# Neighbourhood-attention heads: four single score banks, forms built in quarters, and a fixed TensorE order

## The chip, the cores and the metric

The kernel runs on one core of a Trainium2 chip. The metric is the device time of one execution in microseconds (us); lower is better. The engines that matter here are TensorE (PE), VectorE (DVE), ScalarE (ACT), GpSimd (POOL) and SyncE's DMA queue (SP).

## The reference

A two-layer encoder on x of 1 x 1024 x 1024 in f32. Each layer projects the normalised x once, feeds three groups of token mixers (6 heads of multi-head latent attention, called MLA; 6 heads of 2-D neighbourhood attention; 4 differential heads), gates their outputs, joins them and projects back. The change lies in the neighbourhood heads:

```python
def neighborhood_attention(q, k, v, rpb, scale):        # 64 x 16 grid, window 8 x 16 keys
    ...
    def one(r):
        r0 = jnp.clip(r - kr // 2, 0, rows - kr)
        q_r = lax.dynamic_index_in_dim(qg, r, axis=1, keepdims=False)
        k_r = lax.dynamic_slice_in_dim(kg, r0, kr, axis=1)[:, :, col_idx]
        v_r = lax.dynamic_slice_in_dim(vg, r0, kr, axis=1)[:, :, col_idx]
        ...
        s = jnp.einsum('bchd,brcjhd->bhcrj', q_r, k_r, preferred_element_type=jnp.float32) * scale
        s = s + bias.transpose(0, 2, 1, 3)[None].astype(jnp.float32)
        p = jax.nn.softmax(s.reshape(B, H, GRID_W, kr * kc), axis=-1).reshape(B, H, GRID_W, kr, kc)
        return jnp.einsum('bhcrj,brcjhd->bchd', p.astype(v.dtype), v_r)
```

## The kernel before, in words

Each layer runs latent and differential projections, the differential heads and gates, the neighbourhood projections, the **neighbourhood stage** (6 heads), the MLA stage (6 heads) and the output projection. In the neighbourhood stage a head has 8 tiles of 128 queries; a tile looks at 2 or 3 chunks of 128 keys (`NA_CHUNKS`), so that its score is 128 x 256 or 128 x 384.

The steps of a tile, with their lines before the change:
- **Score** (L1047, L1048): two matmuls into PSUM, because the keys are kept as a high and a low part.
- **Softmax**: DVE adds the bias and takes the minimum of the negated score in one pass (L1052), ACT takes the exponential and its sum (L1053), DVE the reciprocal (L1055), POOL multiplies (L1056).
- **Turn**: PE transposes the probabilities chunk by chunk (L677, in `transpose_plain`) into a T tile in PSUM, and ACT copies it to SBUF (L140, in `copy_act`).
- **Value products** (L1075): after every odd tile, for the pair of tiles that ends there, into an O tile. After tile 7, `finish` (L1084) multiplies them into the gate on DVE.

Ahead of a head stand its **forms**, the transposed queries and keys: four groups of 4 transposes into an F tile (L1018 for the two query halves, L1032 for the two key halves). A query half is finished by ACT (L1019) and then DVE (L1020), a key half by ACT (L140) and then DVE (L1034). A DVE copy (L1027) prepares the keys. `na_table` (L992) loads a head's bias table and prepares it on POOL.

The PSUM tiles: S (`psS`) is two tiles of 1024 columns, each two banks of 512; T is two tiles of one bank, F one and O one, eight banks in all. A score takes a whole S tile, so two scores are in rotation.

What sets the order: the program lists its steps by position, one position per tile (`at`, `run_events`): a score stands `ahead` = 3 positions before its tile, a head's forms `lead` = 4 before the head's first tile and its table `tlead` = 6. From that source order the tile framework's scheduler, with its own estimate of times, decides the order in which each engine gets its instructions; engines run them in that order. `chain(fn)` (L653) makes a step wait in the schedule behind the step chained last, which fixes TensorE's order to the source's; before the change the differential heads use it and the neighbourhood heads don't. `mla_setup` (L1107), with two loads of w_uq (L1114) and their high and low parts on DVE (L1120, L1121), belongs to the MLA stage, and the scheduler puts it among the neighbourhood heads' first tiles. Its two loads share one raw buffer, so the second starts when the first one's DVE work is done.

Of the kernel before, what the change touches and what calls it, by code (L numbers as in the profile page):

```python
# [27 lines left out]
    T=2,  # L28
    hl=(1, 3, 5, 7, 9, 11, 13, 15),
    start="x0 x1 x2 x3 a7 w0 x4 x5 x6 x7 a0 a1 w3 a2 w1 a3 a4 w2 a5 a6", ada="vvvvvvvg", xs=(), hi="A", ks=(0, 1, 7, 2, 3, 4, 5, 6),  # L30
    na=dict(lead=4, tlead=6, ahead=3, delay=0.0, step=0.0),
    late=((0, 8, 0, 12, 4), (0, 0, 0, 8, 0)),
    next=dict(banks="FOFOFOFO", lo=(0, 1, 2, 3)),
    norms=(((0, 2), "V"), ((2, 2), "G")), ropes=((0, 2), (2, 2)), nas=(4, 5), vafter=2,
# [9 lines left out]
def hybrid_encoder_kernel(  # L44
# [81 lines left out]
    def psF():  # L126
        return T(ps_1, "F", [128, 512], F32, bufs=1) if OPT["T"] < 3 else psT()
# [4 lines left out]
    def f(ap):  # L132
        return ap.bitcast(F32)
# [5 lines left out]
    def copy_act(o, i, scale=1.0):  # L139
        A.activation(o, i, AF.Copy, scale=scale)  # L140
# [321 lines left out]
    for l in range(depth):  # L462
# [208 lines left out]
                fn()  # L671
            events.clear()

        def transpose_plain(src_cols, dst, n, act):
            pt = psT()
            for i in range(n):
                ins = PE.transpose(pt[:, i * 128:(i + 1) * 128], src_cols(i), ident)  # L677
            pv = pt[:, 0:n * 128].rearrange("p (k n) -> p k n", n=128)
            if act:
                copy_act(dst, pv)  # L680
            else:
                V.tensor_copy(dst, pv)
            return ins

        def transpose_split(src_cols, hi4, lo4, n):

# [317 lines left out]
            G.tensor_tensor(ti, te, cmask.rearrange("p (d x) -> p d x", x=8).unsqueeze(2).to_broadcast([128, 3, 16, 8]), ALU.add)  # L1004
            return t[:, 384:768], t[:, 0:384]

        def na_forms(h, part=(0, 1)):
            e = h % 2
            hs = slice(h * 64, (h + 1) * 64)
            m, o = (64, 0) if e else (0, 64)  # L1010
            gq = vT[l][m:m + 64, 40:41]
            q, khi, klo = (forms[:, 3 * e + i] for i in range(3))
            ps_ = slice((h // 2) * 128, (h // 2 + 1) * 128)
            for th in range(2 if 0 in part else 0):
                ns = slice(th * 512, (th + 1) * 512)
                ps = psF()
                for t in range(4):
                    PE.transpose(ps[:, t * 128:(t + 1) * 128], nq[:, th * 4 + t, ps_], ident)  # L1018
                A.activation(q[m:m + 64, ns], ps[m:m + 64], AF.Copy, scale=gq)  # L1019
                V.scalar_tensor_tensor(q[o:o + 64, ns], ps[m:m + 64], gq, f(q[m:m + 64, ns]), ALU.mult, ALU.subtract)  # L1020
            if 1 not in part:
                return
            if h == 0:
                kn = rawtile([128, 1024]).rearrange("p (t h d) -> p t h d", h=2, d=64)
            else:
                kn = PTf[e][:, 6:8].rearrange("p a (t h d) -> p (a t) h d", h=2, d=64)
            V.tensor_copy(kn, nk[:, :, hs].unsqueeze(2).to_broadcast([128, 8, 2, 64]))  # L1027
            for th in range(2):
                ns = slice(th * 512, (th + 1) * 512)
                ps = psF()  # L1030
                for t in range(4):
                    PE.transpose(ps[:, t * 128:(t + 1) * 128], kn[:, th * 4 + t].rearrange("p h d -> p (h d)"), ident)  # L1032
                copy_act(khi[:, ns], ps)
                V.tensor_tensor(klo[:, ns], ps, f(khi[:, ns]), ALU.subtract)  # L1034

        def na_item(h, p):
            e, qb, tq = h % 2, p // 4, p % 4
            c0, n = NA_CHUNKS[p]
            w = n * 128
            q, khi, klo = (forms[:, 3 * e + i] for i in range(3))  # L1040
            box = {}

            def first():
                te, ti = na_tabs[h]
                ps = psS()[:, 0:w]
                ks = slice(c0 * 128, c0 * 128 + w)
# [12 lines left out]
                box["p"] = pb  # L1059

            def second():
                pb = box["p"]
                qs = slice(tq * 128, (tq + 1) * 128)
                transpose_plain(lambda i: pb[:, i * 128:(i + 1) * 128], PTf[qb][:, 0:n, qs], n, True)

            def third():

                if p == 1:
                    obox["na", h] = psO()
                O = obox["na", h][:, p // 2 * 128:(p // 2 + 1) * 128]  # L1070
                for i in range(3):
                    for t in (p - 1, p):
                        c, m = NA_CHUNKS[t]
                        if i < m:
                            PE.matmul(O[t % 2 * 64:t % 2 * 64 + 64], nv[:, c + i, h * 64:(h + 1) * 64],  # L1075
                                      PTf[qb][:, i, t % 4 * 128:(t % 4 + 1) * 128], start=(i == 0), stop=(i == m - 1),
                                      skip_group_check=True)

            def finish():
                m = 64 * e  # L1080
                g = sg[m:m + 64, 3 + h // 2].rearrange("p (t two n) -> p two t n", two=2, n=128)
                for half in range(2):
                    O = obox["na", h][half * 64:half * 64 + 64].rearrange("p (t n) -> p t n", n=128)
                    V.tensor_tensor(g[:, half], g[:, half], O, ALU.mult)  # L1084

            return first, second, ([third] if p % 2 else []) + ([finish] if p == 7 else [])

        def nv_side(tt):
            nonlocal forms
            if tt == OPT["nas"][0]:  # L1090
                forms = T(bp, "R0", [128, 8, 1024], F32R)
                na_forms(0, (0,))
            if tt == OPT["nas"][1]:
                na_forms(0, (1,))
# [317 lines left out]
```

## Time and profile before

| | us |
|---|---|
| runs | 1796.34, 1795.14, 1791.98 |
| median of the runs | 1795.14 |
| profiled execution, its own time | 1793.4 |
| its span in the trace | 1789.4 |
| PE busy | 1627.4 (91%) |
| DVE busy | 1305.3 (73%) |
| ACT busy | 902.0 (50%) |
| POOL busy | 782.5 (44%) |

The profiled execution's time is 4.0 us above its span and 1.7 us below the median. The busy shares are averages over all stages. The neighbourhood stage begins with the first score at 526.23 us in layer 0 and at 1393.31 us in layer 1; the first turns of heads 0, 1 and 5 lie at 533.33, 546.40 and 604.00 us in layer 0. A row of the timeline gives start, duration, engine, line and tiles, and in brackets the idle time of the engine before it and the instruction that ended that idle time.

### The profile page before, as it was taken

What the parts mean: (1) busy time and instruction counts of PE and PEld (TensorE: products, weight loads), DVE (VectorE), ACT (ScalarE), POOL (GpSimd) and SP (SyncE); (2) the same over time, 40 slices, a digit from 0 to 9 for tenths busy, and PEclk for the clock granted to TensorE, in tenths of its full rate; (3) what the DMA queues carried; (4) which work ended last, traced back from release to release, by engine and by line L of the source; (5) the groups of instructions that cost most, each with busy time, mean ns of one, the idle gap of its engine ahead of it and who ended that gap; (6) DMA issues with size and microseconds to landing.
All of it is one profiled execution on the core that took longest, in us unless ns stands there. A gap on an engine that the chain in (4) does not pass through costs nothing. (4 is left out here: it accounts for less than half of the span.)

```text
span 1789.4 us, 27407 instructions
## 1 busy us (share of the span) xinstructions
PE 1627.4 (91%) x10028; PEld 1376.8 (77%) x10028; DVE 1305.3 (73%) x2634; ACT 902.0 (50%) x1906; POOL 782.5 (44%) x759
## 2 busy tenths in 40 slices
PE   3999899989989899989998979899899889999998
PEld 2978677768876689878878877777689667897876
DVE  6889877875887589995576477778665666899732
ACT  5622577772127577653342226778511575776500
POOL 4532345544236544473225034455324364456532
PEclk8999899999989999999999999999999999999999
DMA  9335000103333000131232320001032130022032
GB/s 294 99 108 177 14 25 13 48 1 98 116 73 50 36 12 13 36 93 34 83 111 71 90 89 24 13 25 36 25 108 48 21 76 1 13 48 71 13 107 81
DMA packets 135497, 111.68 MB, mean 62 GB/s; under 512 B 32894, under 2 KB 118980, under 8 KB 134852
## 3 DMA queue, kind: packets, MB, share of 16 engines
q1 hardware_dynamic: 119596, 100.33, 19.7%
q0 software_dynamic: 12480, 6.29, 2.2%
q10 hardware_dynamic: 3288, 3.33, 0.9%
q8 instruction: 79, 1.29, 0.3%
q14 instruction: 54, 0.44, 0.1%
HBM read 92.10 MB, written 21.02 MB: 63 GB/s over the span
## 5 line engine op out<-in xcount | busy, mean ns | idle before, releaser
L659 PE MATMUL F<-R,Pb 128*128 128x512 f32 x766 | 232.2, 418 | 15.3 <-ACT sg L140 15.3
L140 ACT ACTIVATE R<-T 128x512 fp32r<-128x512 f32 (+2 forms) x288 | 153.5, 551 | 93.1 <-PE T L689 67.8
L659 PEld LDWEIGHTS F<-R,Pb 128*128 128x128 f32 x766 | 139.9, 195 | 51.4 <-ACT sg L140 22.7
L770 DVE TENSOR_REDUCE sm<-S 128x1 f32<-128x1024 f32 x128 | 153.5, 1217 | 18.4 <-PE S L765 17.2
L1220 POOL TENSOR_SCALAR Pb<-Pb,sm 128x1024 f32<-128x1024 f32 x96 | 109.2, 1138 | 131.8 <-DVE sm L1216 82.1
L692 DVE TENSOR_TENSOR R<-T,R 128x512 fp32r<-128x512 f32 x192 | 128.8, 682 | 24.8 <-ACT R L140 23.4
L1218 ACT ACTIVATE Pb<-S,sm,rs_q 128x1024 f32<-128x1024 f32 x96 | 115.5, 1203 | 40.2 <-DVE sm L1216 34.9
L1238 PE MATMUL O<-R,nd 128*128 128x256 f32 x768 | 120.5, 293 | 8.7 <-DVE R L692 8.1
L1215 DVE TENSOR_REDUCE sm<-S 128x1 f32<-128x1024 f32 x96 | 116.5, 1214 | 8.1 <-PE S L1212 7.7
L689 PE MATMUL T<-ident,Pb 128*128 128x128 f32 x768 | 111.7, 276 | 5.5 <-DVE R L692 5.2
L1238 PEld LDWEIGHTS O<-R,nd 128*128 128x128 f32 x768 | 102.5, 191 | 15.7 <-DVE R L692 11.7
L1344 POOL TENSOR_TENSOR raw<-sg,raw 128x512 fp32r<-128x512 f32 x32 | 50.0, 1562 | 121.0 <-DVE raw L1343 121.0
L689 PEld LDWEIGHTS T<-ident,Pb 128*128 128x128 f32 x768 | 90.4, 143 | 12.1 <-issue 4.1
L772 ACT ACTIVATE nd<-S,sm 128x1024 f32<-128x1024 f32 x64 | 71.4, 1116 | 44.8 <-DVE sm L770 41.3
L776 POOL TENSOR_SCALAR nd<-nd,sm 128x1024 f32<-128x1024 f32 x48 | 58.9, 1228 | 79.3 <-DVE sm L774 76.3
L494 ACT ACTIVATE t<-T 128x512 f32<-128x512 f32 x32 | 19.2, 599 | 143.3 <-DVE n1k L974 68.3
L840 POOL TENSOR_TENSOR Pb<-raw,Pb 128x512 fp32r<-128x512 f32 x32 | 42.1, 1318 | 112.7 <-DVE Pb L839 47.9
L772 ACT ACTIVATE sg<-S,sm 128x1024 f32<-128x1024 f32 x64 | 71.3, 1114 | 29.1 <-DVE sm L770 17.9
L1210 PE MATMUL S<-R 128*128 128x512 f32 x192 | 85.2, 446 | 0.4
L1056 POOL TENSOR_SCALAR Pb<-Pb,sm 128x384 f32<-128x384 f32 (+1 forms) x96 | 53.6, 568 | 59.7 <-DVE sm L1055 48.7
L1211 PE MATMUL S<-R 128*128 128x512 f32 x192 | 78.0, 406 | 0.0
L1212 PE MATMUL S<-R 128*128 128x512 f32 x192 | 77.4, 405 | 0.0
(434 smaller groups left out, 4994.8 us busy)
## 6 DMA issues: line engine op xcount, KB each, us to landing
raw<-in_w_in_dram SPq DMA_DIRECT2D x32, 512.0 KB
t<-in_ada_w_dram SPq DMA_DIRECT2D x40, 256.0 KB
n1k<-in_w_out_dram SPq DMA_DIRECT2D x16, 512.0 KB
v_d<-n1k SPq DMA_DIRECT2D x16, 384.0 KB
nl<-in_ada_w_dram SPq DMA_DIRECT2D x24, 256.0 KB
nd<-v_d POOLq DMA_DIRECT2D x12, 512.0 KB, 5.1
R<-in_ada_w_dram SPq DMA_DIRECT2D x8, 512.0 KB
Pb<-in_x_dram SPq DMA_DIRECT2D x8, 512.0 KB
```

The costliest lines, as they stand in the source:

```text
L140: A.activation(o, i, AF.Copy, scale=scale)
L659: ins = fn()
L689: PE.transpose(pt[:, i * 128:(i + 1) * 128], src_cols(i), ident)
L692: V.tensor_tensor(lo4, pv, f(hi4), ALU.subtract)
L770: V.tensor_reduce(stt[:, m:m + 1], ps, AX.X, ALU.max, negate=True)
L772: A.activation(p, ps.rearrange("p (k n) -> p k n", k=8), AF.Exp, bias=stt[:, m:m + 1], accum_out=stt[:, 2 + m:3 + m])
L1210: PE.matmul(o, qhi[:, ts_], khi[:, ks], start=True, stop=False)
L1211: PE.matmul(o, qhi[:, ts_], klo[:, ks], start=False, stop=False)
L1215: V.tensor_reduce(stt[:, 0:1], ps, AX.X, ALU.max, negate=True)
L1218: A.activation(p, ps, AF.Exp, bias=stt[:, 3:4], scale=rs, accum_out=stt[:, 1:2])
L1220: mla["g"] = G.tensor_scalar(p, p, stt[:, 2:3], 0.0, ALU.mult, ALU.add)
L1238: PE.matmul(box["o"], mla[f"v{e}"][:, k], mla["PT"][b][:, hl, k], start=(k == 0 and hl == 0), stop=(k == 7 and hl == 1))
```

## The change

- **Score banks**: two S tiles are taken once for the stage and cut into four single banks of 512 columns; scores rotate through these (`na_s`). `ahead` goes from 3 to 4.
- **Forms in quarters**: `na_forms` builds one quarter per call (query half 0, query half 1, key half 0, key half 1). The quarters of heads 1 to 5 are listed 1.25 positions apart, the first 9 positions before the head's first tile (`lead` from 4 to 9); `tlead` goes from 6 to 10. Head 0's quarters stand where its forms stood.
- **Order**: the transposes of a turn, the scores, the value products and the quarters of heads 1 to 5 go through `chain`, so TensorE gets the whole stage in source order.
- `transpose_plain` loses a choice of engine that was always ACT here.

```diff
-    na=dict(lead=4, tlead=6, ahead=3, delay=0.0, step=0.0),
+    na=dict(lead=9, tlead=10, ahead=4, delay=0.0, step=0.0),
...
-        def transpose_plain(src_cols, dst, n, act):
+        def transpose_plain(src_cols, dst, n):
             pt = psT()
-            for i in range(n):
-                ins = PE.transpose(pt[:, i * 128:(i + 1) * 128], src_cols(i), ident)
...
+            def pe():
+                for i in range(n):
+                    ins = PE.transpose(pt[:, i * 128:(i + 1) * 128], src_cols(i), ident)
+                return ins
+
+            chain(pe)
+            copy_act(dst, pt[:, 0:n * 128].rearrange("p (k n) -> p k n", n=128))
...
-        def na_forms(h, part=(0, 1)):
+        def na_forms(h, side, th, order):
...
+            ns, ps = slice(th * 512, (th + 1) * 512), psF()
...
+            order(pe)
+            if side:
+                copy_act(khi[:, ns], ps)
+                V.tensor_tensor(klo[:, ns], ps, f(khi[:, ns]), ALU.subtract)
+            else:
                 A.activation(q[m:m + 64, ns], ps[m:m + 64], AF.Copy, scale=gq)
                 V.scalar_tensor_tensor(q[o:o + 64, ns], ps[m:m + 64], gq, f(q[m:m + 64, ns]), ALU.mult, ALU.subtract)
...
-                ps = psS()[:, 0:w]
+                ps = na_s()[:, 0:w]
...
-                PE.matmul(ps, q[:, p * 128:(p + 1) * 128], khi[:, ks], start=True, stop=False)
-                PE.matmul(ps, q[:, p * 128:(p + 1) * 128], klo[:, ks], start=False, stop=True)
+                def pe():
+                    PE.matmul(ps, q[:, p * 128:(p + 1) * 128], khi[:, ks], start=True, stop=False)
+                    return PE.matmul(ps, q[:, p * 128:(p + 1) * 128], klo[:, ks], start=False, stop=True)
+
+                chain(pe)
...
+                chain(pe)
...
+        banks = [psS() for _ in range(2)]
+        na_s = Ring([t[:, a:a + 512] for t in banks for a in (0, 512)])
...
             if h:
-                at(p - o["lead"], lambda: na_forms(h))
+                for i in range(4):
+                    at(p - o["lead"] + i * 1.25, partial(na_forms, h, i // 2, i % 2, chain))
```

The `chain(pe)` that stands alone is that of the value products in `third`. In the changed kernel the lines are: score L1054 and L1055, bias and minimum L1061, exponential L1062, reciprocal L1064, turn L679, value products L1086, transposes of the forms L1027, query half ACT L1035 and DVE L1036, key half DVE L1033, w_uq's parts L1139 and L1140.

Three places show what the change does to the order of an engine's instructions.

**DVE at the stage's start, layer 0.** F is a tile of head 1's forms, S a score, t the raw w_uq, nd its parts. Before:

```order
L1121 SCALAR_TENSOR_TENSOR nd_5586<-t_674_5587,vT_19_109,nd_5586 128x6x16 [waits DVE_49] x2
L1020 SCALAR_TENSOR_TENSOR R_491_4567<-F_4814,vT_19_109,R_491_4567 64x512 [waits Activation_49]
L1055 RECIPROCAL sm_4716<-sm_4716 128x1 [waits Activation_49]
L1052 ISA Pb_4704,sm_4732<-S_4729,t_507_4707 128x384 [waits PE_49]
L1052 ISA sm_4732 128x1
L1052 ISA Pb_4704,sm_4740<-S_4737,t_507_4707 128x384 [waits PE_49]
L1052 ISA sm_4740 128x1
L1055 RECIPROCAL sm_4724<-sm_4724 128x1 [waits Activation_49]
L1052 ISA Pb_4704,sm_4752<-S_4749,t_507_4707 128x384 [waits PE_49]
L1052 ISA sm_4752 128x1
L1055 RECIPROCAL sm_4732<-sm_4732 128x1 [waits Activation_49]
L1120 TENSOR_SCALAR nd_5586<-t_675_5595,vT_19_109 128x6x96 [waits DMAHW7_49]
```

Now:

```order
L1139 TENSOR_SCALAR nd_5549<-t_632_5558,vT_19_109 128x6x96 [waits DMAHW7_49]
L1139 TENSOR_SCALAR nd_5549<-t_632_5558,vT_19_109 128x6x16
L1061 ISA Pb_4704,sm_4744<-S_4708,t_509_4709 128x384 [waits PE_49]
L1061 ISA sm_4744 128x1
L1139 TENSOR_SCALAR nd_5549<-t_632_5558,vT_19_109 128x6x16
L1140 SCALAR_TENSOR_TENSOR nd_5549<-t_632_5558,vT_19_109,nd_5549 128x6x96 [waits DVE_49]
L1140 SCALAR_TENSOR_TENSOR nd_5549<-t_632_5558,vT_19_109,nd_5549 128x6x16 [waits DVE_49] x2
L1061 ISA Pb_4704,sm_4758<-S_4707,t_509_4709 128x384 [waits PE_49]
L1061 ISA sm_4758 128x1
L1036 SCALAR_TENSOR_TENSOR R_491_4567<-F_4749,vT_19_109,R_491_4567 64x512 [waits Activation_49]
```

The second w_uq load's parts (t_632, waiting for the DMA queue), two bias passes and the parts' second half now stand ahead of the DVE step that finishes head 1's first query half (F_4749); before, that step (F_4814) stood ahead of them. In layer 1 the rows read alike.

**PE around the last tile of a head.** T_5212 before and T_5053 now are the turns of a head's tile 7. Before:

```order
L677 MATMUL T_5212<-ident_76,Pb_4704 128x128 [waits PE_49,Pool_49]
L677 MATMUL T_5212<-ident_76,Pb_4704 128x128
L1075 MATMUL O_5086<-R_506_4706,n1v_3937 64x128 [waits Activation_49]
L1047 MATMUL S_5204<-R_491_4567 128x384 [waits DVE_49]
L1048 MATMUL S_5204<-R_491_4567 128x384
L1075 MATMUL O_5086<-R_506_4706,n1v_3937 64x128 [waits Activation_49]
L1075 MATMUL O_5086<-R_506_4706,n1v_3937 64x128 x3
L1047 MATMUL S_5223<-R_491_4567 128x384 [waits DVE_49]
L1048 MATMUL S_5223<-R_491_4567 128x384 [waits DVE_49]
L1018 MATMUL F_5300<-ident_76,n1q_3381 128x128 [waits PE_49]
L1018 MATMUL F_5300<-ident_76,n1q_3381 128x128 x3
L1047 MATMUL S_5235<-R_491_4567 128x384 [waits DVE_49]
```

Now:

```order
L1027 MATMUL F_5046<-ident_76,n1q_3381 128x128 x4
L679 MATMUL T_5053<-ident_76,Pb_4704 128x128 [waits PE_49,Pool_49]
L679 MATMUL T_5053<-ident_76,Pb_4704 128x128
L1086 MATMUL O_4948<-R_506_4706,n1v_3937 64x128 [waits Activation_49] x2
L1086 MATMUL O_4948<-R_506_4706,n1v_3937 64x128 x3
L1054 MATMUL S_4707<-R_491_4567 128x384
L1055 MATMUL S_4707<-R_491_4567 128x384
L1027 MATMUL F_5071<-ident_76,n1q_3381 128x128 [waits DVE_49]
L1027 MATMUL F_5071<-ident_76,n1q_3381 128x128 x3
L679 MATMUL T_5078<-ident_76,Pb_4704 128x128 [waits Pool_49]
L679 MATMUL T_5078<-ident_76,Pb_4704 128x128
L1054 MATMUL S_4707<-R_491_4567 128x384 [waits DVE_49]
```

Before, the products that wait for ACT are issued in pieces with other work between them; now a pair's products stand directly behind the turn of its second tile, and the next form's transposes stand in a fixed place behind them.

**ACT at the same tiles.** Before:

```order
L140 ACTIVATE R_506_4706<-T_5199 128x3x128 [waits PE_49,Activation_49]
L140 ACTIVATE R_491_4567<-F_5160 128x512 [waits PE_49]
L140 ACTIVATE R_506_4706<-T_5212 128x2x128 [waits PE_49,Activation_49]
L1053 ACTIVATE Pb_4704,sm_5175<-Pb_4704,sm_5175 128x256 [waits DVE_49]
L1053 ACTIVATE Pb_4704,sm_5194<-Pb_4704,sm_5194 128x384 [waits DVE_49,Activation_49]
L1053 ACTIVATE Pb_4704,sm_5207<-Pb_4704,sm_5207 128x384 [waits DVE_49,Activation_49]
```

Now:

```order
L140 ACTIVATE R_506_4706<-T_5034 128x3x128 [waits PE_49,Activation_49]
L1062 ACTIVATE Pb_4704,sm_5023<-Pb_4704,sm_5023 128x384 [waits DVE_49,Activation_49]
L1035 ACTIVATE R_491_4567<-F_5046,vT_19_109 64x512 [waits PE_49]
L1062 ACTIVATE Pb_4704,sm_5041<-Pb_4704,sm_5041 128x384 [waits DVE_49]
L140 ACTIVATE R_506_4706<-T_5053 128x2x128 [waits PE_49,Activation_49]
L1035 ACTIVATE R_491_4567<-F_5071,vT_19_109 64x512 [waits PE_49]
```

Before, the copy of tile 7's turn (T_5212) stood ahead of the exponentials; now it (T_5053) stands behind an exponential, a query half's step (F_5046) and another exponential.

## Rows read from the trace of the kernel before

**Rows 1.** The page, part 1: busy us, share of the span, instructions.
```profile
PE 1627.4 (91%) x10028; PEld 1376.8 (77%) x10028; DVE 1305.3 (73%) x2634; ACT 902.0 (50%) x1906; POOL 782.5 (44%) x759
```

**Rows 2.** Timeline of PE: first turns of heads 0, 1, 5; heads 1, 5 of layer 1.
```profile
533.33 0.41 PE L677 MATMUL T<-ident,Pb 128*128 128x128 f32 x1
546.40 0.44 PE L677 MATMUL T<-ident,Pb 128*128 128x128 f32 x2
604.00 0.33 PE L677 MATMUL T<-ident,Pb 128*128 128x128 f32 x1
1416.72 0.27 PE L677 MATMUL T<-ident,Pb 128*128 128x128 f32 x1
1474.17 0.33 PE L677 MATMUL T<-ident,Pb 128*128 128x128 f32 x1
```

**Rows 3.** Timeline of PE inside one head (start us, us).
```profile
540.54 0.66 PE L1032 MATMUL F<-ident,R 128*128 128x128 f32 x4
540.96 0.54 PE L1048 MATMUL S<-R 128*128 128x256 f32 x2
542.12 0.55 PE L677 MATMUL T<-ident,Pb 128*128 128x128 f32 x3
542.42 0.42 PE L1047 MATMUL S<-R 128*128 128x384 f32 x1
542.95 0.87 PE L1075 MATMUL O<-R,n1v 128*64 128x128 f32 x10
543.75 0.44 PE L677 MATMUL T<-ident,Pb 128*128 128x128 f32 x2
```

**Rows 4.** Groups of instructions by line, whole run (busy, mean ns, idle before).
```profile
L1047 PE MATMUL S<-R 128*128 128x384 f32 (+1 forms) x96 | 38.3, 416 | 8.7 <-DVE sm L1052 7.1 <-ACT R L140 1.4
L1075 PE MATMUL O<-R,n1v 128*64 128x128 f32 x528 | 56.2, 286 | 4.3 <-ACT R L140 4.0 <-DVE sg L1084 0.2
L1018 PE MATMUL F<-ident,n1q 128*128 128x128 f32 x96 | 15.5, 286 | 3.5 <-DVE R L1020 2.2 <-POOL n1q L988 1.3
```

**Rows 5.** Groups by line, stretch 540 to 604 us.
```profile
L1053 ACT ACTIVATE Pb<-Pb,sm 128x384 f32<-128x384 f32 (+1 forms) x37 | 21.6, 584 | 3.4 <-DVE sm L1055 1.7 <-DVE sm L1052 1.2
L140 ACT ACTIVATE R<-T 128x384 f32<-128x384 f32 (+1 forms) x36 | 15.9, 458 | 7.9 <-PE T L677 7.6
L1019 ACT ACTIVATE R<-F,vT 64x512 fp32r<-64x512 f32 x8 | 5.4, 680 | 1.9 <-PE F L1018 1.7
L1034 DVE TENSOR_TENSOR R<-F,R 128x512 fp32r<-128x512 f32 x9 | 6.2, 687 | 3.7 <-ACT R L140 3.7
L1020 DVE SCALAR_TENSOR_TENSOR R<-F,vT,R 64x512 fp32r<-64x512 f32 x8 | 6.0, 750 | 0.3
```

**Rows 6.** Timeline of PE: a turn, and the products that follow it.
```profile
602.50 0.89 PE L677 MATMUL T<-ident,Pb 128*128 128x128 f32 x5
603.63 0.43 PE L1075 MATMUL O<-R,n1v 128*64 128x128 f32 x2 [0.23 <-ACT R L140]
```

**Rows 7.** Stage start: PE, SP, DMA rate in 40 slices of 530 to 535, DVE.
```profile
531.73 1.11 PE L1018 MATMUL F<-ident,n1q 128*128 128x128 f32 x4 [2.19 <-DVE R L1020]
530.91 0.34 SPq L1114 DMA_DIRECT2D t<-in_w_uq_dram  x1
GB/s 0 0 0 0 0 0 0 0 0 0 0 0 0 0 0 184 111 55 92 111 258 350 442 277 240 203 37 0 0 0 0 0 0 0 0 0 0 0 0 0
534.12 1.11 DVE L1120 TENSOR_SCALAR nd<-t,vT 128x576 fp32r<-128x576 f32 x3
535.15 0.54 DVE L1052 CUSTOM_DVE_ANT_0 Pb<-S,t 128x384 f32<-128x384 f32 x1
536.52 0.82 DVE L1121 SCALAR_TENSOR_TENSOR nd<-t,vT,nd 128x576 fp32r<-128x576 f32 x1
```

**Rows 8.** Windows at the stage's start and inside a head: busy by engine, PEclk.
```profile
532.00:536.00 4.00, 4.00 (x21) 3.31 (x20) 3.42 (x14) 3.43 (x10) 1.90 (x3) 0.67 0.23 68
556.00:560.00 4.00, 2.51 (x17) 1.52 (x12) 3.89 (x13) 2.04 (x6) 1.47 (x3) 1.00 0.00 0
```

More of the change, by code (lines that the diff above doesn't have):

```diff
@@ L1013, in na_forms @@
             ps_ = slice((h // 2) * 128, (h // 2 + 1) * 128)
-            for th in range(2 if 0 in part else 0):
-                ns = slice(th * 512, (th + 1) * 512)
-                ps = psF()
-                for t in range(4):
-                    PE.transpose(ps[:, t * 128:(t + 1) * 128], nq[:, th * 4 + t, ps_], ident)
+            ns, ps = slice(th * 512, (th + 1) * 512), psF()
+            if side and th == 0:
+                if h == 0:
+                    kn = rawtile([128, 1024]).rearrange("p (t h d) -> p t h d", h=2, d=64)
+                else:
+                    kn = PTf[e][:, 6:8].rearrange("p a (t h d) -> p (a t) h d", h=2, d=64)
+                V.tensor_copy(kn, nk[:, :, hs].unsqueeze(2).to_broadcast([128, 8, 2, 64]))
+                na_kn[0] = kn
+            def pe():
+                for t in range(4):
+                    src = na_kn[0][:, th * 4 + t].rearrange("p h d -> p (h d)") if side else nq[:, th * 4 + t, ps_]
+                    ins = PE.transpose(ps[:, t * 128:(t + 1) * 128], src, ident)
+                return ins
+            order(pe)
+            if side:
+                copy_act(khi[:, ns], ps)
+                V.tensor_tensor(klo[:, ns], ps, f(khi[:, ns]), ALU.subtract)
+            else:
                 A.activation(q[m:m + 64, ns], ps[m:m + 64], AF.Copy, scale=gq)
                 V.scalar_tensor_tensor(q[o:o + 64, ns], ps[m:m + 64], gq, f(q[m:m + 64, ns]), ALU.mult, ALU.subtract)
[L1021 to L1034, printed above, removed]
+        na_kn = [None]
+        now = lambda fn: fn()
         def na_item(h, p):
@@ L1044, in first, with pe @@
                 te, ti = na_tabs[h]
-                ps = psS()[:, 0:w]
+                ps = na_s()[:, 0:w]
                 ks = slice(c0 * 128, c0 * 128 + w)
-                PE.matmul(ps, q[:, p * 128:(p + 1) * 128], khi[:, ks], start=True, stop=False)
-                PE.matmul(ps, q[:, p * 128:(p + 1) * 128], klo[:, ks], start=False, stop=True)
+                def pe():
+                    PE.matmul(ps, q[:, p * 128:(p + 1) * 128], khi[:, ks], start=True, stop=False)
+                    return PE.matmul(ps, q[:, p * 128:(p + 1) * 128], klo[:, ks], start=False, stop=True)
+                chain(pe)
                 tb = te[:, 128:384] if p == 0 else te[:, 0:256] if p == 7 else ti
@@ L1063, in second @@
                 qs = slice(tq * 128, (tq + 1) * 128)
-                transpose_plain(lambda i: pb[:, i * 128:(i + 1) * 128], PTf[qb][:, 0:n, qs], n, True)
+                transpose_plain(lambda i: pb[:, i * 128:(i + 1) * 128], PTf[qb][:, 0:n, qs], n)
             def third():
@@ L1070, in third, with pe @@
                 O = obox["na", h][:, p // 2 * 128:(p // 2 + 1) * 128]
[L1071 to L1077, printed above, removed]
+                def pe():
+                    for i in range(3):
+                        for t in (p - 1, p):
+                            c, m = NA_CHUNKS[t]
+                            if i < m:
+                                ins = PE.matmul(O[t % 2 * 64:t % 2 * 64 + 64], nv[:, c + i, h * 64:(h + 1) * 64],
+                                                PTf[qb][:, i, t % 4 * 128:(t % 4 + 1) * 128], start=(i == 0), stop=(i == m - 1),
+                                                skip_group_check=True)
+                    return ins
+                chain(pe)
             def finish():
@@ L1091, in nv_side @@
                 forms = T(bp, "R0", [128, 8, 1024], F32R)
-                na_forms(0, (0,))
+                for th in range(2):
+                    na_forms(0, 0, th, now)
             if tt == OPT["nas"][1]:
-                na_forms(0, (1,))
+                for th in range(2):
+                    na_forms(0, 1, th, now)
         forms = None
```

6 lines of the change are left out of this document (removed).

## The prediction

> **What bounds the kernel now.** I read the page first: PE is busy 91% of the span [rows 1], so a change that moves the time must move PE's busy time or its waits. The change touches the neighbourhood stage alone, so I then read the timeline of PE there and took the first turn of each head as a milestone. From head 1 to head 5 it goes from 546.40 to 604.00 us in layer 0 and from 1416.72 to 1474.17 in layer 1 [rows 2]: 57.60 and 57.45 us for four heads, **14.4 us per head** in both. No instruction is added to PE or taken from it, so the question is which part of 14.4 is work and which is waiting.
>
> The work is read from distances between starts on PE where nothing waits [rows 3]: a wide score pair 0.53 (542.42 to 542.95), ten value products 0.80 (542.95 to 543.75), a turn of three chunks 0.30 (542.12 to 542.42), a form's four transposes 0.42 (540.54 to 540.96). A head has 8 scores (two narrow ones, so 0.50 each), 8 turns (0.30 in front of a score, more in front of a product; I take 0.35), 44 products and 4 forms: 8 x 0.50 + 8 x 0.35 + 44 x 0.08 + 4 x 0.40 = 4.0 + 2.8 + 3.4 + 1.6 = **11.8 us**. So a head holds some 2.6 us of waits in this way of counting. The groups by line say what they are [rows 4]: over both layers PE sat idle 8.7 us before scores, 7.1 of it for DVE's pass over an earlier score (the two-deep S ring), 4.3 before value products for ACT's copy of a turn, 3.5 before the query halves' transposes. This is less than 2.6 per head, since the tail of a matmul counts as busy.
>
> **The change, part by part.**
>
> *Four score banks, scores four tiles ahead.* This takes away the wait of 7.1 us over both layers [rows 4], some 0.6 per head. A score then finds a bank that DVE left long ago.
>
> *The fixed order: value products right behind their turn.* Before, other work stood between; now products follow the turn of their own odd tile at once, as the PE rows of the change show, and wait for ACT's copy. What that costs is seen where before happens to do the same [rows 6]: five transposes start at 602.50 and need 0.5 to issue, the products start at 603.63, so 0.6 is lost, of which only 0.23 shows as idle. Tiles 3 and 5 now have this: 2 x 0.6 = 1.2. Tile 1 has a form's transposes between and I count nothing for it. At tile 7 ACT has more ahead of the copy, by its own rows of order: the query half of the next head (0.68), an exponential (0.58), then the copy (0.46) [rows 5], together 1.7 after the form's transposes, of which the turn itself covers 0.2: 1.5.
>
> *Forms in quarters, one F bank, fixed places.* Each quarter's transposes wait until the quarter before has left the bank, through ACT and then DVE. Second query half to first key half: 0.68 + 0.75 [rows 5] and two handovers, some 1.75, against 1.05 of PE work between them (turn, score, turn): 0.7. First to second key half: ACT's copy (some 0.6 for its 512 columns, by the 0.46 for 384), DVE's 0.69 with a bias pass of 0.54 [rows 5, 7] ahead of it, and an exponential (0.58) ahead on ACT: 2.4, against 1.2 of PE work: 1.2.
>
> So the waits per head come to 1.2 + 1.5 + 0.7 + 1.2 = **4.6**, and the period to 11.8 + 4.6 = 16.4, which is 2.0 over 14.4. Four heads in each of two layers: **+16**. Both ends: if ACT is free whenever a turn ends (tile 7 at 0.6) and nothing stands ahead of the forms (0.5 and 0.3), waits are 2.6 and the term is 0; if each of tiles 3 and 5 finds an exponential ahead of its copy, they are 5.8 and the term is +26. I take 4.6 since ACT's rows put an exponential or a form between most copies.
>
> *The stage's start.* The rows of DVE's order show the second w_uq load's parts moved ahead of the step that finishes head 1's first query half. PE is chained: the second query half's transposes wait for that step, and the first turn stands behind them. The load is issued when the first load's parts are done, at 530.91 [rows 7]; with one bias pass (0.54) less ahead, at 530.4. In the rate of its packets the last slice with traffic is the 27th of 0.125 us, so it ends at 533.4, 2.5 after its issue. DVE then starts on it at 532.9 and runs 1.11 for the high parts, 0.82 and some 0.55 for the low ones, two bias passes of 0.54, and the query half of 0.75: until 537.2. The transposes then take 0.8 at the clock granted there (531.73 to the next start at 532.52 before), so the first turn lies near 538.4 instead of 533.33 [rows 2]: +5.1. Before, PE idled 2.19 for the same kind of step [rows 7], so this is an old wait grown longer. Layer 1 has the same order of rows: **+10** for both, between 8 and 12. Who waits behind: all chained turns and so ACT's copies.
>
> *The rest.* The first head runs without a head's overlap before it: +1, between -4 and +5, since a head that starts late finds its softmax done. End of the stage: 0, between -5 and +5, as MLA's first work fills gaps there. POOL keeps its order but for a place or two; on SP only the load of one head's bias table moves behind a rope table's, with half a head to spare: nothing; without that cover one load's 2.5 us per layer.
>
> **Sum:** 16 + 10 + 1 = +27 on the profiled execution's 1793.4 (its span of 1789.4 and 4.0 around it), so 1820.4. The median of the runs lies 1.7 above it: **1822 us**.
>
> A rule that speaks against my sum: the Trainium skill, page "Perfetto Trace Analysis", section "Matmuls", says that independent groups of matmuls should rotate through different PSUM banks, so that ACT or DVE empties one while the next group runs. By it the change is right, and the time would be that of the first rival. The trace bears it out for the 7.1 us of waits on the two-deep ring, which I give up above.
>
> **The rivals.**
>
> *Faster: the waits go and none takes their place.* If ACT reaches each copy within the time that a turn takes to issue, only the single F bank's wait of some 0.6 is left, and a head takes 12.4. Ten periods of 2.0 less, with the first heads', are -20, the start still costs +10: 1793.4 - 10 + 1.7 = **1785**. For it: ACT is busy 50% on average [rows 1], and the largest group of waits is the one that goes. Against it: the row of products behind a turn [rows 6] and ACT's order at tile 7. It decides where the waits fall under 1.6 per head: a period of 13.4, ten times 1.0, just repays the start.
>
> *No change: waits of 1.6 to 2.0 per head*, so that new waits replace the old ones and the start is paid by the first heads, which then find softmax and forms ready: **1795**, within 5.
>
> *Slower still: the clock falls inside the heads.* At the start, after the idle 2.19, PE was granted 0.67 of its clock from 532 to 536 [rows 7, 8], that is a mix of its two levels, 1.2 and 2.4 GHz. Inside a head a stretch with PE busy only 2.51 of 4 us kept 1.00 [rows 8], so one wait of that kind doesn't lower it; the change makes more of them. If every head has one such stretch of 4 us at 0.67, it loses 4 x 0.33 = 1.3, and twelve heads lose 16: **1838**. The Trainium skill, page "TensorE: Matmul & The Clock Gate", section "A second HAM failure mode: psum-queue depth-cycling", tells of a kernel whose frequent micro-idles between groups of matmuls made the clock swing between its levels. The row from 556 to 560 us speaks against it here, the one from 532 to 536 for it.
>
> That the change doesn't do what it says is left out: PE's rows in their new order show the scores in two held tiles and the quarters apart.
>
> **How the numbers follow.** Forecast 0.62, slower still 0.19, faster 0.11, no change 0.08. A measurement of this kernel tells some 0.3% from nothing, 5.4 us. The forecast and the slower rival lie above 1800.5: slower 0.81; same 0.08; faster 0.11. The range leaves out the faster rival, about half of no change and the far end of slower still: from 1796, where the period's term is near 0 and the start is partly repaid, to 1846, which takes in the term's upper end (+26 instead of +16) and a lower clock. The forecast's own range is 1806 to 1834.
>
> **What would show it.** In the changed kernel's profile: the first turn 12 us after the first score rather than 7; first turns 16.4 apart; idle time of PE before scores near 1 for DVE; before value products, for ACT, 10 to 20 rather than 4.3; before the forms' transposes, for DVE, 15 to 30; PE's busy time near 1627; the clock at 1.00 inside the heads. I am wrong if first turns stand 13.4 apart or less, or if the first turn of a layer isn't late; the slower rival holds if the granted clock inside the heads is well under 1.

## The result and the profile after

The changed kernel takes **1820.19 us** (median of 4 runs, 1819.4 to 1822.71) against 1793.87 before on the same terms: a ratio of **1.0146**, 95% interval 1.0130 to 1.0162. It is slower, by about what was forecast. The profiled execution took 1819.52 with a span of 1817.7, that is 28.3 more than the span before (1789.4).

The rows below are first turns of heads 0, 1 and 5 in layer 0, and of heads 1 and 5 in layer 1 (timeline of PE in the changed kernel: start, duration, engine, line), which answer to [rows 2]:

```profile
540.70 0.42 PE L679 MATMUL T<-ident,Pb 128*128 128x128 f32 x1
557.05 0.27 PE L679 MATMUL T<-ident,Pb 128*128 128x128 f32 x1
627.93 0.27 PE L679 MATMUL T<-ident,Pb 128*128 128x128 f32 x1
1437.23 0.27 PE L679 MATMUL T<-ident,Pb 128*128 128x128 f32 x1
1507.85 0.27 PE L679 MATMUL T<-ident,Pb 128*128 128x128 f32 x1
```

From head 1 to head 5 it now takes 70.88 and 70.62 us, 17.7 per head where it was 14.4. The groups of PE by line over the whole run (busy, mean ns, idle before and who ended it), which answer to [rows 4]:

```profile
L1086 PE MATMUL O<-R,n1v 128*64 128x128 f32 x528 | 55.7, 285 | 17.0 <-ACT R L140 17.0
L1054 PE MATMUL S<-R 128*128 128x384 f32 (+1 forms) x96 | 41.7, 435 | 20.9 <-DVE sm L1061 20.9
L1027 PE MATMUL F<-ident,n1q 128*128 128x128 f32 x96 | 16.3, 298 | 8.3 <-DVE R L1036 7.0 <-POOL n1q L988 1.2
L1027 PE MATMUL F<-ident,R 128*128 128x128 f32 x80 | 13.4, 293 | 9.5 <-DVE R L1033 7.0 <-DVE R L1036 2.3
```

The wait before products (L1086) rose from 4.3 to 17.0, as the sum had it. The wait before scores (L1054) did not vanish: it **rose** from 8.7 to 20.9. The next stretch shows why (timeline of PE and DVE around the end of head 0):

```profile
551.48 0.44 PE L1054 MATMUL S<-R 128*128 128x384 f32 x1
552.25 0.56 DVE L1061 CUSTOM_DVE_ANT_0 Pb<-S,raw 128x384 f32<-128x384 f32 x1 [0.76 <-PE S L1055]
552.87 0.44 PE L1054 MATMUL S<-R 128*128 128x384 f32 x1 [0.44 <-DVE sm L1061]
...
556.15 0.45 PE L1054 MATMUL S<-R 128*128 128x384 f32 x1
557.68 0.56 DVE L1061 CUSTOM_DVE_ANT_0 Pb<-S,raw 128x384 f32<-128x384 f32 x1
558.30 0.44 PE L1054 MATMUL S<-R 128*128 128x384 f32 x1 [0.88 <-DVE sm L1061]
```

The score at 552.87 starts when DVE has passed over the score just before it (551.48), and the one at 558.30 likewise waits for the pass over 556.15, which DVE starts late because the last step of head 0 (`finish`, 1.38 us from 556.27) stands ahead of it. So every second score waits for its neighbour, not for the one four tiles back. The rows of PE's order quoted with the change already had it: of two scores into S_4707 the first has no wait, the second waits for DVE. The order treats the two halves of a held tile as one; the first experiment tests this.

The wait at tile 7 is the one that was worked out (timeline of ACT and PE):

```profile
553.97 0.68 ACT L1035 ACTIVATE R<-F,vT 64x512 fp32r<-64x512 f32 x1 [0.34 <-PE F L1027]
554.55 0.60 ACT L1062 ACTIVATE Pb<-Pb,sm 128x384 f32<-128x384 f32 x1
555.15 0.37 ACT L140 ACTIVATE R<-T 128x256 f32<-128x256 f32 x1
555.57 0.66 PE L1086 MATMUL O<-R,n1v 128*64 128x128 f32 x8 [1.06 <-ACT R L140]
```

ACT runs a form's step, an exponential and only then the copy; the products go on at 555.57, after 1.06 us of idle time. At the stage's start (PE and DVE, answering to [rows 7]):

```profile
530.76 0.44 PE L1054 MATMUL S<-R 128*128 128x384 f32 x1 [1.67 <-DVE sm L1061]
534.14 0.66 PE L1054 MATMUL S<-R 128*128 128x384 f32 x1 [2.42 <-DVE sm L1061]
539.82 1.09 PE L1027 MATMUL F<-ident,n1q 128*128 128x128 f32 x4 [3.21 <-DVE R L1036]
...
530.63 1.01 DVE L1140 SCALAR_TENSOR_TENSOR nd<-t,vT,nd 128x576 fp32r<-128x576 f32 x1
533.44 0.55 DVE L1061 CUSTOM_DVE_ANT_0 Pb<-S,t 128x384 f32<-128x384 f32 x1
535.87 0.70 DVE L1139 TENSOR_SCALAR nd<-t,vT 128x576 fp32r<-128x576 f32 x2 [0.81 <-DMA t<-in_w_uq_dram]
538.92 0.76 DVE L1036 SCALAR_TENSOR_TENSOR R<-F,vT,R 64x512 fp32r<-64x512 f32 x1
```

The first score is at 528.61 and the first turn at 540.70: 12.1 us instead of 7.1, as forecast, but in three waits. In the first two a second half waits for DVE's pass over the first half, and that pass stands behind the first w_uq load's parts (for the second wait L1140 from 530.63, the pass only at 533.44); the forecast knew of the third wait alone.

The sum of what moved in the span, in us, from these and the same rows of layer 1 and MLA:

| stretch | layer 0 | layer 1 |
|---|---|---|
| before the first score (same order of PE; the time around the span fell by 2.2) | +2.4 | |
| first score to first turn | +5.0 | +5.2 |
| head 0 | +3.3 | -0.1 |
| heads 1 to 4 | +13.3 | +13.2 |
| first turn of head 5 to MLA's first score | -4.8 | -5.0 |
| from there to the next layer's first score, or the end | -3.7 | -0.4 |

The end of the stage gives back some 5 us per layer. MLA's work now stands among the last head's turns: MLA's first score, at 633.70 in layer 0, comes 8.8 us ahead of the last transpose of a turn (642.49); before, it came 0.6 behind it (614.61 and 614.04).

### The profile page after: what moved, and what is told of

It is laid out like the page before. It is cut to its first block, busy times and chain, and to the rows that moved or that the text cites. A ratio compares the mean times of both kernels' runs of the same rounds, so it can differ in the third digit from the quotient of the medians.

```text
span 1817.7 us, 27423 instructions
## 1 busy us (share of the span) xinstructions
PE 1623.9 (89%) x10028; PEld 1376.2 (76%) x10028; DVE 1313.2 (72%) x2634; ACT 904.2 (50%) x1906; POOL 782.0 (43%) x759
## 5 line engine op out<-in xcount | busy, mean ns | idle before, releaser
L659 PEld LDWEIGHTS F<-R,Pb 128*128 128x128 f32 x766 | 141.1, 196 | 51.9 <-ACT sg L140 22.8
L770 DVE TENSOR_REDUCE sm<-S 128x1 f32<-128x1024 f32 x128 | 153.6, 1217 | 20.9 <-PE S L765 19.6
```

What stands on the lines that cost most here:

```text
L659: ins = fn()
L770: V.tensor_reduce(stt[:, m:m + 1], ps, AX.X, ALU.max, negate=True)
```

## The experiments

Ratios are to the kernel before, run on the same chip, with 95% intervals. A and B are the theory and the rival that each expectation sets against each other.

**Alternating banks.** Consecutive scores into different tiles.

```diff
-        na_s = Ring([t[:, a:a + 512] for t in banks for a in (0, 512)])
+        na_s = Ring([t[:, a:a + 512] for a in (0, 512) for t in banks])
```

> The changed kernel with the four score banks taken in another order: first halves of both held tiles, then second halves. Theory A (a score into the second half of a held tile waits for DVE's pass over the first half of the same tile, so the four banks act as two): consecutive scores then lie in different tiles, PE's idle time before scores falls from 20.9 us to 8 or less, first turns of heads stand some 16.5 apart rather than 17.7; head 1's first query half also moves ahead of the second w_uq load's parts on DVE, which gives some 3 per layer back at the start. Sum: some 1806 us. Rival B (scores wait because DVE itself is behind, with forms and copies ahead of its passes): idle before scores stays at 15 or more, and only the start's gain shows: some 1814.

Measured 1815.22, ratio 1.0118 (1.0090 to 1.0146). Groups of PE by line:

```profile
L1086 PE MATMUL O<-R,n1v 128*64 128x128 f32 x528 | 56.7, 294 | 25.3 <-ACT R L140 24.8
L1054 PE MATMUL S<-R 128*128 128x384 f32 (+1 forms) x96 | 42.1, 439 | 3.6 <-DVE sm L1061 3.6
L1027 PE MATMUL F<-ident,R 128*128 128x128 f32 x80 | 14.2, 307 | 15.8 <-DVE R L1036 15.8
```

The mechanism is A's: the scores' wait falls from 20.9 to 3.6, and first turns of heads stand 16.6 apart. The time is B's (A had some 1806): products now wait 25.3, and the key halves 15.8. The first turn comes 7.4 and 8.5 us after the first score instead of 12.1, but head 0 is longer by 3.4 and 1.1. While products stand right behind their turn, PE hands the wait on.

**Products one position later.**

```diff
-    na=dict(lead=9, tlead=10, ahead=4, delay=0.0, step=0.0),
+    na=dict(lead=9, tlead=10, ahead=4, delay=1.0, step=0.0),
```

> The changed kernel with the value products one position later (delay 1.0), so that a turn of the next tile and a score lie between a turn and its products. Theory A (the fixed order exposes ACT's copy): PE's idle time before products falls from 17.0 to under 3, first turns stand some 16.3 apart rather than 17.7, and the time falls by some 12, to 1808. Rival B (PE only hands its wait to the next instruction in the chain, which waits for the same ACT): the wait before products falls but turns, scores or forms take it up, and the time stays within 3 of 1820.

Measured 1794.99, ratio 1.0006 (0.9987 to 1.0024): the whole loss, some 25 us, is gone by one number. Groups of PE by line:

```profile
L1086 PE MATMUL O<-R,n1v 128*64 128x128 f32 x528 | 45.5, 282 | 0.5
L1054 PE MATMUL S<-R 128*128 128x384 f32 (+1 forms) x96 | 41.0, 427 | 7.6 <-DVE sm L1061 7.6
L1027 PE MATMUL F<-ident,n1q 128*128 128x128 f32 x96 | 16.5, 300 | 21.2 <-DVE R L1036 19.9 <-POOL n1q L988 1.2
```

First turns stand 13.2 apart on average (13.7, and 11.6 for the last). A holds and was too small: with 16.5 us of waits before products went 13.3 of the scores' wait. As I read it, a PE that waits for ACT issues its next score late, and DVE's pass, the exponential and the next copy come late with it; this was not tried apart. Part of the wait is handed on, as B has it: the query halves' rises from 8.3 to 21.2. The first turn stays 12.0 us behind the first score.

**No chain.** `chain(pe)` is `pe()` in turns, scores and products, and the quarters are placed by the scheduler; banks, lead and quarters stay.

```diff
-            chain(pe)
+            pe()
```

> The changed kernel without the chain: banks, lead, quarters as they are, but the scheduler orders PE in the neighbourhood stage. Theory A (the fixed order carries the loss): first turns stand 14 to 15 apart again and the time is 1795, within 5. Rival B (the quarters with their single F bank and the two-halves banks carry it): spacing stays at 16 or more and the time at 1810 or more.

Measured 1797.13, ratio 1.0015 (0.9997 to 1.0032); first turns of heads 1 to 5 stand 15.1 apart on average. A: with PE's order free, the same banks and quarters cost nothing that the measurement tells.

**Chain alone.** The same chain for turns, scores and products in the kernel before; forms free and all at once, whole S tiles. For the scores, and for turns and products likewise:

```diff
-                PE.matmul(ps, q[:, p * 128:(p + 1) * 128], khi[:, ks], start=True, stop=False)
-                PE.matmul(ps, q[:, p * 128:(p + 1) * 128], klo[:, ks], start=False, stop=True)
+                def pe():
+                    PE.matmul(ps, q[:, p * 128:(p + 1) * 128], khi[:, ks], start=True, stop=False)
+                    return PE.matmul(ps, q[:, p * 128:(p + 1) * 128], klo[:, ks], start=False, stop=True)
+
+                chain(pe)
```

> The kernel before with one part of the change alone: turns, scores and value products of the neighbourhood stage go through the chain; the forms all at once and unchained, two whole S tiles, lead, ahead and tlead as before. Theory A (products that stand right behind their turn in a fixed order carry the loss): PE's idle time before products for ACT rises from 4.3 us to 12 or more, first turns of heads stand 16 or more apart, the time is 1808 to 1820. Rival B (the fixed order costs little by itself; the quarters and the halves of a held tile carry it): products wait under 8 us, spacing 14 to 15, the time within 5 of 1795.

Measured 1797.08, ratio 1.0007 (0.9990 to 1.0025): B for the time. Products wait 9.8, between A's 12 and B's 8, and scores 2.0:

```profile
L1082 PE MATMUL O<-R,n1v 128*64 128x128 f32 x528 | 59.4, 294 | 9.8 <-ACT R L140 7.8 <-DVE sg L1094 0.4
L1051 PE MATMUL S<-R 128*128 128x384 f32 (+1 forms) x96 | 41.5, 433 | 2.0 <-DVE sm L1058 2.0
```

The spacing is A's: first turns of heads 1 to 5 stand 16.5 apart. What lengthens it is the last step, 22.8 and 22.4 us, and this is repaid: MLA's first score comes 8.7 and 5.6 us later after the stage's first score than before, and the stretch from there to the next layer's first score, or the end, is 8.2 and 6.3 shorter. So the spacing of heads alone doesn't tell the time.

Neither the chain by itself nor the rest by itself makes the kernel slower by more than the measurement tells; the loss is in the two together.

**Quarters out of the chain**, in the changed kernel (`now` runs a step at once, without the chain, so that the scheduler places it).

```diff
-                    at(p - o["lead"] + i * 1.25, partial(na_forms, h, i // 2, i % 2, chain))
+                    at(p - o["lead"] + i * 1.25, partial(na_forms, h, i // 2, i % 2, now))
```

> The changed kernel with the forms' quarters out of the chain, nothing else: turns, scores and products stay in the fixed order, and the scheduler places the quarters' transposes (it puts two of a head's four between a turn and its products). Theory A (a fixed order without anything between a turn and its products exposes ACT's copy; filling two of the four places takes half of it away): idle before products falls from 17.0 us to 8 to 12, idle before scores stays above 10, heads 15.5 to 16.5 apart, the time 1805 to 1812. Rival B (the quarters' fixed places are the whole loss): the time is within 5 of 1795. Rival C (they are none of it): within 4 of 1820.

Measured 1803.34, ratio 1.0040 (1.0022 to 1.0058); first turns stand 16.7 apart. Products wait 8.4, scores 22.3:

```profile
L1086 PE MATMUL O<-R,n1v 128*64 128x128 f32 x528 | 60.0, 289 | 8.4 <-ACT R L140 8.4
L1054 PE MATMUL S<-R 128*128 128x384 f32 (+1 forms) x96 | 41.5, 433 | 22.3 <-DVE sm L1061 21.4 <-ACT R L1035 0.8
```

A, nearly to its numbers: quarters that the scheduler may put between a turn and its products take back some 1% of the 1.5%. The wait of the halves of a tile stays; that the remaining 0.4% is its price was not shown.

**The second w_uq load's parts held** behind head 1's query halves, in the changed kernel (`na_hold` is the DVE step of the second query half).

```diff
+                with ExitStack() as held:
+                    if kc:
+                        held.enter_context(tc.issue_after(na_hold[0]))
```

> The changed kernel with the second w_uq load's parts held on DVE behind head 1's query halves, nothing else. Theory A (these parts make the first turn late): the first turn comes some 8 us after the first score in both layers rather than 12.1, and the time falls by 8 to 10, to some 1811. Rival B (a late start is repaid by the heads behind it, which find more softmax done): the first turn is early but the time is 1817 or more.

Measured 1822.27, ratio 1.0155 (1.0116 to 1.0195): B, though this interval is too wide to tell a gain of some 4 us from none. The timeline of PE has the waits of the start again:

```profile
530.91 0.44 PE L1057 MATMUL S<-R 128*128 128x384 f32 x1 [1.89 <-DVE sm L1064]
534.09 0.66 PE L1057 MATMUL S<-R 128*128 128x384 f32 x1 [2.22 <-DVE sm L1064]
538.11 1.09 PE L1027 MATMUL F<-ident,n1q 128*128 128x128 f32 x4 [1.54 <-DVE R L1036]
```

Only the third wait shrank, from 3.21 to 1.54; the first turn comes 10.4 and 9.9 us after the first score, where both theories had it earlier (A at some 8), and head 0 is 0.7 and 1.0 longer. From the first score to the stage's last turn it takes 115.1 and 113.8 us, against 113.9 and 113.7 in the changed kernel: the 1.7 and 2.3 us are repaid within the stage.

**Late products, both loads held, and the banks' order.** Products one position late; both w_uq loads' parts held behind head 1's last quarter; banks alternating in the first run, in the change's order in the second.

```diff
-    na=dict(lead=9, tlead=10, ahead=4, delay=0.0, step=0.0),
+    na=dict(lead=9, tlead=10, ahead=4, delay=1.0, step=0.0),
...
-                V.tensor_tensor(klo[:, ns], ps, f(khi[:, ns]), ALU.subtract)
+                ins = V.tensor_tensor(klo[:, ns], ps, f(khi[:, ns]), ALU.subtract)
+                if h == 1:
+                    na_hold[0] = ins.ins
...
+                with tc.issue_after(na_hold[0]):
```

In the first run also:

```diff
-        na_s = Ring([t[:, a:a + 512] for t in banks for a in (0, 512)])
+        na_s = Ring([t[:, a:a + 512] for a in (0, 512) for t in banks])
```

> The changed kernel with three edits: products one position later, score banks taken alternately from the two tiles, and both w_uq loads' parts held on DVE behind head 1's last quarter. Theory A (what the late products leave is the start, where DVE works on w_uq and scores wait for passes over the other half): the first turn comes some 7 us after the first score rather than 12, first turns stay 13.7 apart or less, the time is 1780 to 1787, below the kernel before. Rival B (the start is repaid by the first heads, as holding the second load's parts alone showed): the first turn is early, the first head longer by as much, and the time stays within 4 of 1795.

> The changed kernel with products one position later and both w_uq loads' parts held, score banks in the change's own order (both halves of one tile, then of the other). Theory A (two halves of a tile are one for the order, which still costs): PE idles 7 us or more before scores and the time is 4 or more above the run with banks taken alternately. Rival B (with late products, DVE's passes come early enough that the order of the banks does not matter): both within 3 us of each other.

Measured 1786.23, ratio 0.9952 (0.9932 to 0.9972), with alternating banks, and 1798.48, ratio 1.0019 (1.0000 to 1.0038), without. The scores of the first run, then of the second:

```profile
L1057 PE MATMUL S<-R 128*128 128x384 f32 (+1 forms) x96 | 39.5, 412 | 0.6 <-DVE sm L1064 0.6
```

```profile
L1057 PE MATMUL S<-R 128*128 128x384 f32 (+1 forms) x96 | 40.5, 422 | 6.0 <-DVE sm L1064 5.9
```

A in both, but for scores that wait 6.0 and not 7 or more: the order of the same four banks is worth 12 us here, and the first of the two is faster than the kernel before. Of the 12, 8.5 lie before head 2's first turn, which comes 34.2 and 34.5 us after the first score instead of 39.5 and 37.8; from there on heads stand alike in both (13.6 to 13.7 us apart, the last 11.6 to 11.9). Why the order matters only to the first heads was not tried.

Holding the parts, without alternating, gave nothing (ratio 1.0019 against the 1.0006 of late products alone), and it shows a start that is repaid. These are the first turns of head 0 with late products alone, and with the parts held as well:

```profile
538.54 0.42 PE L679 MATMUL T<-ident,Pb 128*128 128x128 f32 x1
536.84 0.27 PE L679 MATMUL T<-ident,Pb 128*128 128x128 f32 x1
```

The first scores are at 526.56 and 529.94, so the first turn comes 6.9 us after the first score instead of 12.0 (6.7 instead of 12.0 in layer 1). But heads 0 and 1 are longer by nearly as much: head 2's first turn comes 39.5 and 37.8 us after the first score, against 39.3 in both layers.

**Quarters further apart.** The first of those two, with quarters 2 positions apart from 11 ahead, and with 1.5 from 10.

```diff
-    na=dict(lead=9, tlead=10, ahead=4, delay=1.0, step=0.0),
+    na=dict(lead=11, tlead=11, ahead=4, delay=1.0, step=0.0),
...
-                    at(p - o["lead"] + i * 1.25, partial(na_forms, h, i // 2, i % 2, chain))
+                    at(p - o["lead"] + i * 2, partial(na_forms, h, i // 2, i % 2, chain))
```

> The same three edits, and the quarters 2 positions apart rather than 1.25, the first 11 positions ahead of the head (tables as well). Theory A (the one F bank makes the quarters' transposes wait when they stand close, 1.64 us once per head in the kernel with late products): PE's idle time before the forms' transposes falls below 6 us, heads stand some 12.5 apart, the time is some 8 below the run without this edit, 1772 to 1780. Rival B (ACT and DVE are full enough that the wait moves to scores or turns): spacing stays at 13.5 and the time within 3 of the run without it.

> The run with late products, alternating banks and held w_uq parts, with quarters 1.5 positions apart from 10 ahead instead of 1.25 from 9. Theory A (the F bank's wait of 1.64 between the query quarters goes when a score, a turn and a product pair stand between them): spacing some 13.0, the time some 4 below that run. Rival B (the wait moves to products, as with quarters 2 apart): within 2 of it.

Measured 1785.50, ratio 0.9946 (0.9926 to 0.9967), and 1787.17, ratio 0.9944 (0.9923 to 0.9965): B in both, for the time. At 2 apart the waits of the query and key halves fell to 5.9 and 5.8, but the products' came back to 9.3; at 1.5 the wait moved from the query halves (5.3) to the key halves (23.1).

**Products two positions late**, with quarters 2 apart, and the same without `tc.issue_after(na_hold[0])`.

```diff
-    na=dict(lead=11, tlead=11, ahead=4, delay=1.0, step=0.0),
+    na=dict(lead=11, tlead=11, ahead=4, delay=2.0, step=0.0),
```

> The run with quarters 2 positions apart, with products two positions late rather than one. Theory A (the 9 us of idle time before products there come from copies that stand behind exponentials on ACT; one more tile in between covers them): idle before products under 2, heads some 12.3 apart, the time some 8 below that run. Rival B (ACT sets the pace by then): the idle time moves to turns or scores, spacing stays above 13, the time within 3 of it.

> The fastest run so far (alternating banks, quarters 2 apart, products two positions late) without holding the w_uq parts, which so come back among the first tiles on DVE, ahead of head 1's query halves. Theory A (these parts cost what the first turn is late, some 4 to 5 us in each layer, once nothing behind them waits longer): the first turn comes some 8 to 9 us after the first score instead of 5 to 6, the time is 1776 to 1780. Rival B (the first heads repay it): within 3 of 1770.

Measured **1769.61**, ratio **0.9854** (0.9834 to 0.9873), and 1771.37, ratio 0.9877 (0.9850 to 0.9904) without holding. Groups of PE in the first:

```profile
L679 PE MATMUL T<-ident,Pb 128*128 128x128 f32 x264 | 45.8, 279 | 5.4 <-POOL Pb L1068 5.4
L1089 PE MATMUL O<-R,n1v 128*64 128x128 f32 x528 | 43.7, 287 | 1.0 <-DVE sg L1101 1.0
L1057 PE MATMUL S<-R 128*128 128x384 f32 (+1 forms) x96 | 40.1, 418 | 0.0
L1027 PE MATMUL F<-ident,n1q 128*128 128x128 f32 x96 | 14.7, 276 | 8.6 <-DVE R L1038 4.7 <-DVE R L1033 1.4 <-DVE sm L1067 1.4
```

First turns stand 13.0 apart on average, down to 10.8; the time fell by some 16 us where A had 8, and part of the idle time moved to the turns, which now wait 5.4 for POOL. With next to no wait before scores or products, the change's three ideas, so arranged, beat the kernel before by 1.5%. Holding the parts did not matter as far as the measurement tells (0.9854 and 0.9877, whose intervals overlap; B): without it the first turn is 7.1 and 8.5 us after the first score instead of 4.7 and 6.4, and head 1 is 2.6 and 2.1 shorter.

## Why the prediction came out

The forecast time was 1822 and the sign, the size and the spacing's direction were right; two of its terms were wrong in opposite directions, and that they cancel is luck.

- **Products behind their turn**: right. Forecast 10 to 20 us of idle time before them, measured 17.0, and at tile 7 the queue on ACT that the order's rows showed. Putting one tile between gives back 25 us, the whole loss and more than the term said.
- **Scores**: wrong. The step "A score then finds a bank that DVE left long ago" failed. The idle time was forecast near 1 and measured 20.9, because the order makes the second half of a held tile wait for the pass over the first. The wait stood in the quoted rows and was not read. Alternating tiles, which takes it to 3.6, shows the cause.
- **Forms in quarters**: right. The forecast was 15 to 30 us idle before their transposes for DVE; measured were 7.0 + 7.0 + 2.3, at the lower end.
- **Heads**: 16.4 us apart was forecast, 17.7 measured, so the term is +26.5 and not +16, at the upper end given for it. With alternating tiles, which take most of the scores' wait away, heads stand 16.6 apart; so that wait accounts for most of the difference, although other waits grew there. (In the sum of a head's work, 44 x 0.08 is 3.5 and not 3.4.)
- **Start**: the size held (+5.1 forecast per layer, 5.0 and 5.2 measured), the cause half. The second load's parts account for one of three waits; holding them brought the first turn 1.7 and 2.3 us forward and gained no time that could be told. The other two are waits of second halves for passes that stand behind the first load's parts. Alternating tiles, and likewise holding both loads' parts, took most of the 5 us away. The steps given for the start also add up to 538.0 and not 538.4, so that its size was met by some luck. And the start was not worth its +10: with late products, 5 us less of it in each layer gained nothing.
- **End of the stage**: "0, between -5 and +5" was at its end, -4.8 and -5.0, and layer 0's MLA gave 3.7 more: from head 3's to head 4's first score there took 34.8 us before and 31.2 now, as in layer 1 in both kernels. Before, one wait of 1.89 before products lies in it, and the granted clock falls behind it (timeline of PE, and a window with the columns of [rows 8], which the next point explains; the granted clock of 0.64 is a mix of the two levels):

```profile
738.56 0.63 PE L1238 MATMUL O<-R,nd 128*128 128x256 f32 x3 [1.89 <-DVE R L692]
740.00:744.00 4.00, 4.00 (x20) 3.83 (x19) 3.03 (x10) 1.87 (x4) 1.76 (x2) 0.64 0.00 0
```

  Such a wait and the 34.8 us stand again in layer 0 of the run with products two positions late, so the 3.7 need not come from the change. What brings that wait was not tried.
- **Clock**: the rival "slower still" did not come: the windows of the changed kernel show the granted clock near half (0.58 and 0.50) at the start alone, and 1.00 in the heads of both layers from there on, in spite of their many short waits. The columns, as in [rows 8], are the length, the busy us (and instructions) of PE, of its weight loads, of DVE, ACT and POOL, the granted clock as a share of the higher level, the DMA share and GB/s.

```profile
532.00:536.00 4.00, 1.86 (x7) 1.79 (x8) 2.46 (x11) 1.31 (x4) 2.15 (x4) 0.58 0.27 74
536.00:540.00 4.00, 0.79 (x3) 0.31 (x3) 3.87 (x13) 2.10 (x5) 0.04 (x1) 0.50 0.00 0
544.00:560.00 16.00, 12.53 (x93) 9.28 (x94) 9.78 (x31) 10.05 (x27) 6.08 (x12) 1.00 0.10 13
560.00:576.00 16.00, 11.38 (x88) 8.37 (x87) 8.79 (x27) 9.62 (x25) 6.40 (x12) 1.00 0.10 14
```

The Trainium skill's rule on rotating PSUM banks (page "Perfetto Trace Analysis", section "Matmuls") did not decide the sign, but the runs agree with it once the order lets the banks rotate: alternating tiles took the scores' wait from 6.0 to 0.6 and the time down by 12 us, where products were late.

So the sum came out by errors that cancel: heads 10.5 too cheap, the end of the stage and MLA 13.9 too dear, and some 5 too little for what lies before head 1, 2.2 of which the time around the span takes back.

## What to carry to other kernels

When an engine's order is fixed by hand, put a step that waits for another engine's answer at least one tile behind the step that asks for it; nobody fills the gap any more. Read from the program's order rows which waits a new buffer really loses: banks cut from one tile may still be one for the order, and taking the halves of two tiles alternately is a change of one line. A wait at a stage's start that later work repays is worth nothing; test it before paying for it.

## What was not expected of the hardware

In the fastest run the granted clock falls twice inside the heads of layer 0, where it kept 1.00 in the changed kernel. These are windows of the run with products two positions late, then one of the same without holding the parts (columns as in [rows 8]):

```profile
544.00:560.00 16.00, 14.22 (x113) 11.63 (x110) 13.21 (x40) 12.07 (x34) 7.19 (x14) 0.89 0.10 14
576.00:592.00 16.00, 13.74 (x113) 10.94 (x112) 12.33 (x40) 12.62 (x34) 11.73 (x17) 0.91 0.21 71
544.00:560.00 16.00, 15.29 (x141) 12.83 (x140) 13.16 (x41) 13.74 (x37) 8.13 (x17) 1.00 0.20 26
```

It is not that a busier PE gets less: the last row has PE busy 15.29 of 16 us at 1.00, and the changed kernel 11.38 of 16 at 1.00. What PE did before each fall is one longer wait (timeline of PE in the fastest run):

```profile
547.30 0.66 PE L1027 MATMUL F<-ident,R 128*128 128x128 f32 x4 [1.78 <-DVE R L1038]
588.29 0.44 PE L679 MATMUL T<-ident,Pb 128*128 128x128 f32 x2 [1.85 <-POOL Pb L1068]
```

The clock falls about 1 us after the end of each, from the higher level to half. In the changed kernel no wait of PE in heads 1 to 4 is longer than 1.62 us. But in layer 1 of the fastest run waits of 1.78 and 1.87 us at the same places were followed by no fall, so that the wait alone doesn't decide, and the cause stays open.
